# A hybrid decoder layer: half of x turned by the host, small roots moved to VectorE, and a new order of the first weight splits of the last product

## The chip, the cores and the metric

The kernel runs on one core of one Trainium2 chip. The core has five engines that run side by side: TensorE (PE, matrix products and transposes), VectorE (DVE), ScalarE (ACT), GpSimd (POOL) and SyncE (SP, which here only issues transfers). 16 DMA engines move data between the device memory and the on-chip memories SBUF (128 partitions) and PSUM (where TensorE writes). The metric is the device time of one execution in microseconds (us); lower is better. Three runs of the kernel before took 2543.54, 2546.9 and 2548.43 us.

## The reference, cut to what matters

One decoder layer over 2048 tokens of width 1024, all in float32:

```python
h = rms_norm(x, norm1_g)
proj = h @ w_in                       # columns are shared out among three mixers
o_a = swa_sink_mixer(qa, ka, va, ...) # sliding window of 128, learned sinks
o_b = s5_mixer(u, ...)                # complex diagonal state space, 32 groups, GELU and GLU
o_c = nsa_mixer(qc, kvc, gc, ...)     # compressed + selected + window attention, gated
mixed = concat(rms_norm(o_a), rms_norm(o_b), rms_norm(o_c))
x = x + mixed @ w_out
h2 = rms_norm(x, norm2_g)
x = x + relu(h2 @ w_up) ** 2 @ w_down
```

The output is x, 2048 x 1024. `rms_norm` divides by the root of the mean square, so it needs one reciprocal root for each token and part.

## The kernel before, in words

Every product is made from pairs of numbers: an operand is split into a high part that TensorE takes fast (type fp32r) and a low part, the rest. `split` (L1418 to L1421) is the helper: ScalarE casts the high part (L1420), VectorE subtracts it from the source (L1421). A product then is three matmuls: high by high, high by low, low by high.

The order of the instructions on each engine, and of the transfers on each queue, is fixed when the program is built: a planner takes the program in its written order as priority, takes an instruction as soon as its inputs and its buffer are free by its own estimate of times, and can so hoist loads far ahead. `tc.high_priority(offset=n)` moves a block n steps forward in that order. On the chip each engine and each queue runs its list strictly in order, and an instruction that waits holds up all behind it on the same engine or queue.

**`phase_front`** (L81) makes `x @ w_in`. The tokens are taken in 16 tiles of 128 (tile s holds tokens s, s+16, ...). `fetch(s)` loads raw rows (L104). `load_h(s)` turns a tile: eight transposes on TensorE into two PSUM banks (L116), and for each half the split into `hh` (ScalarE, L118) and `hl` (VectorE, L119). The function that it returns squares the raw rows on ScalarE with a sum (L123) and takes the reciprocal root on POOL (L125, in `rsqrt_steps`, L44 to L49: eight small steps, one after another). The root is applied when a product is copied out of PSUM (L172, L176). The 16 tiles go in two halves of eight. Products of the first half come first; then `load_h(8)` to `load_h(15)` are put between the products of chunk `v`, at every second place, and merged with `pair_steps` (L472), which builds tables for the state space mixer: `outer(b)` multiplies on POOL (L483) and VectorE (L484) and adds on POOL (L485); `local(b)` stores the result, makes the small products `pk` (L493) and stores `kst` (L498). Buffers: `ot` has one, `oCA` two, `kst` one, the turned banks two, raw x three. Rows of the finished products for the attention mixers are stored from SP's queue by `store` (L180).

**Attention and the state space mixer** follow. Their bias tables come by `bias_steps`, whose first load is `Ts` (L719), and the weights of the GLU by `glu_steps` (L626), all on SP's queue.

**`phase_mix`** (L1024) is the third mixer, 16 blocks of 128 tokens, and beside it `mixed @ w_out` block by block. `logits` (L860 on) leaves a softmax that POOL scales (L887 on `sls` and `slw`, L1140 on `slc`); `pv` transposes it (L900) and multiplies (L911). `open_late` (L1055) runs once, when the state space mixer is done: it takes the roots `ra` and `rc` of 128x16 sums on POOL, 14 steps each, halves `rc` (L1072), and sends `rc` through memory to turn it. For each block `finish_steps` loads `mix`, scales it on POOL (L1238) and calls `normed` (L934): ScalarE squares with a sum, the root is taken on POOL, and POOL scales (L941). The last block does both on VectorE.

**`phase_up` and `phase_down`** are the FFN. Each product of 2 x 2 blocks is made as seven products instead of eight (Strassen's scheme in Winograd's form); `ORDER = "1675243"` is the order of the seven. `phase_up` ends with combinations on POOL (`ev`, L1582) that are stored to `vd`. `phase_down` (L1667) multiplies `vd` by combinations of `w_down`. For each of eight chunks `weights` makes the differences on POOL (L1723) and `keep` splits the seven weights (`dw`); `tokens(k)` loads the rows for product k from `vd` (L1741) and splits them (`v`). The first chunk's weights and the first five row tiles are written ahead, under high priority, so that they run while `phase_up` ends:

```python
first["0"]()
for k in range(AHEAD):
    tokens(k)
    first[ORDER[k]]()
for o in ORDER[AHEAD:]:
    first[o]()
```

Weights "1" and "6" have a pool of their own (`w_low`), the others share `w_high` (five buffers); rows share `vr` (three raw buffers) and five split buffers. These pools lie where `phase_up` had its own, and each buffer waits for what used its place.

Of the kernel before, what the change touches and what calls it, by code (L numbers as in the profile page):

```python
# [80 lines left out]
def phase_front(tc, C, x, norm1_g, w_in, u_st, pd, rh_a, prm, dkp, dca, pre, extra, done):  # L81

    nc = tc.nc
    with ExitStack() as ctx:
# [14 lines left out]
        r_of, raw_x, hs = {}, {}, {}  # L99

        def fetch(s):
            if s < T16:
                raw_x[s] = xp.tile([P, D], F32, tag="x", name=f"x{s}", bufs=3)
                nc.sync.dma_start(raw_x[s], xv[s])  # L104

        def load_h(s):
# [4 lines left out]
            hs[s] = hh, hl
            for half in range(2):
                pt = ps_t.tile([P, 4, P], F32, tag="pt", name=f"pt{s}_{half}")
                for j in range(4):
                    k = 4 * half + j
                    nc.tensor.transpose(pt[:, j], xt[:, k * P:(k + 1) * P], C["ident"])  # L116
                sl = slice(4 * half, 4 * half + 4)
                nc.scalar.copy(hh[:, sl], pt)  # L118
                nc.vector.tensor_tensor(hl[:, sl], pt, hh[:, sl], op=ALU.subtract)  # L119
# [35 lines left out]
        def product(s, W, ch, k0=0, k1=NK, between=()):  # L155
            kind, c0, n = ch
            hh, hl = hs[s]
            if k0 == 0:
                open_[s, ch] = ps_m.tile([P, n], F32, tag="pm", name=f"pm{s}_{kind}{c0}")
            pm = open_[s, ch]  # L160
            between = list(between)
            for k in range(k0, k1):
                mm3(nc, pm, hh[:, k], hl[:, k], W[k][0], W[k][1], k == 0, k == NK - 1)
                if between:
                    between.pop(0)()
            if k1 < NK:
                return
            if kind == "u":
                r = T16 - 1 - s
                g0 = (c0 - 512) // 16  # L170
                dst = u_st[:, g0:g0 + 16, (r // 8) * P + (r % 8) * 16:(r // 8) * P + (r % 8) * 16 + 16]
                nc.scalar.activation(dst, pm.rearrange("p (g q) -> p g q", q=16), AF.Copy, scale=r_of[s])  # L172
            else:
                f, nh, step = HEADS[kind]
                o = sp.tile([P, n + nh], F32, tag="po", name=f"po{s}_{kind}", bufs=3)
                nc.scalar.activation(o[:, 0:n], pm, AF.Copy, scale=r_of[s])  # L176
                sq = sp.tile([P, 6, 64], F32, tag="sq", name=f"sq{s}_{kind}", bufs=1)[:, 0:nh]
                nc.scalar.activation(sq, o[:, f:f + nh * step].rearrange("p (h d) -> p h d", d=step)[:, :, 0:64], AF.Square)
                nc.vector.tensor_reduce(o[:, n:n + nh], sq, axis=AX.X, op=ALU.add)
                rows.append(lambda: nc.sync.dma_start(pdv[kind][s], o))  # L180
                store(1)
# [290 lines left out]
def pair_steps(tc, C, S, dkp, dca, tp, ps):  # L472
# [5 lines left out]
    def outer(b):  # L478
# [6 lines left out]
        nc.gpsimd.tensor_tensor(CA, CA, t1, op=ALU.add)  # L485
# [361 lines left out]
class Attn:  # L847
# [86 lines left out]
    def normed(self, dst, o, name, eng=None):  # L934
# [5 lines left out]
        rsqrt_into(nc, self.sm, r, ss, 1.0 / 256, 1, "nq", eng)  # L940
# [83 lines left out]
def phase_mix(tc, C, x, gains, B, cmp, w_out, out_norm_g, g2, pd, oa_d, ob, x1, hT, xs, rr, rh, ss_a, ss_b, r_d, rest, release):  # L1024
    nc = tc.nc
    kcA, kcB, vc = cmp
    with ExitStack() as ctx:
# [390 lines left out]
def split(nc, dh, dl, src):  # L1418

    nc.scalar.copy(dh, src)  # L1420
    nc.vector.tensor_tensor(dl, src, dh, op=ALU.subtract)  # L1421
# [245 lines left out]
def phase_down(tc, x1, w_down, vd, out):  # L1667
# [8 lines left out]
    with ExitStack() as ctx:  # L1676
# [12 lines left out]
        acc, V, R = {}, {}, {}  # L1689
# [24 lines left out]
        def weights(c, res):  # L1714
# [20 lines left out]
        def tokens(k):  # L1735
# [7 lines left out]
            split(nc, t[:, 0], t[:, 1], r)  # L1743
# [42 lines left out]
        with tc.high_priority(offset=DOWN_HOIST):  # L1786
# [35 lines left out]
def trunk(tc, x, norm1_g, w_in, qk_g, sinks, rel_bias, a_re, a_im, log_dt, b_re, b_im, c_re, c_im, d_skip, glu_w, glu_b,  # L1822
# [3 lines left out]
    with ExitStack() as ctx:  # L1826
# [38 lines left out]
        phase_front(tc, C, x, norm1_g, w_in, u_st, pd, rh_a, (a_re, a_im, log_dt, b_re, b_im, c_re, c_im, d_skip), dkp, dca,  # L1865
# [93 lines left out]
```

## Time and profile before

| | |
|---|---|
| median of three runs | 2546.9 us |
| the profiled execution, its own time | 2552.13 us |
| its span, first to last instruction | 2550.2 us |
| TensorE busy, matmuls | 2444.3 us, 96% of the span |
| VectorE, ScalarE, GpSimd busy | 1721.8, 1324.6, 1203.2 us |

The same by stage, from the busy time of each engine in stretches of the profile (us):

| stretch | what runs | length | PE | DVE | ACT | POOL | PE clock |
|---|---|---|---|---|---|---|---|
| 0 to 145 | first half of x @ w_in | 145 | 134.89 | 84.02 | 65.90 | 20.23 | 1.00 |
| 145 to 230 | second half turned, pair steps | 85 | 80.29 | 34.85 | 37.92 | 59.88 | 1.00 |
| 230 to 417 | rest of x @ w_in, state space | 187 | 185.72 | 135.32 | 92.85 | 42.46 | 1.00 |
| 417 to 676 | window attention, GLU, compression | 259 | 238.86 | 171.57 | 167.96 | 73.73 | 0.95 |
| 676 to 725 | hand-over inside `phase_mix` | 49 | 37.69 | 30.43 | 28.19 | 23.94 | 0.86 |
| 725 to 1290 | sparse attention and w_out | 565 | 523.50 | 405.39 | 330.86 | 276.36 | 0.97 |
| 1290 to 1929 | first FFN product | 639 | 630.88 | 347.89 | 346.00 | 395.62 | 1.00 |
| 1929 to 2551 | second FFN product | 622 | 612.49 | 512.37 | 254.95 | 310.98 | 0.99 |

How to read the rows further down: a row of the busy view gives a stretch, its length, then for PE, PEld (weight loads), DVE, ACT and POOL the busy time with the number of instructions, the granted clock of TensorE as a share of full speed, the busy share of the DMA engines and the GB/s moved. A row in order of time has the start, the time taken, the engine, the line, the operation, the output and the inputs, how many instructions are merged, and in brackets the idle time before and what ended it. Names are the program's without numbers; L is a line of the kernel before. Matmuls are pipelined, so the time of one is longer than the distance between two.

### The profile page before, as it was taken

The page shows a single profiled execution, that of the slowest core. Times are in us where ns is not written, and L with a number is a line of the kernel's source. Part 1 is how long each engine was busy: PE and PEld are TensorE (multiplying, and loading weights), DVE is VectorE, ACT ScalarE, POOL GpSimd, SP SyncE. Part 2 cuts the span into 40 slices and gives each one's busy share as a digit, 9 for nine tenths or more (in the row PEclk, how much of TensorE's full clock was granted, in tenths as well). Part 3 has the DMA queues.
Part 4 walks back from the last instruction along what each step waited for, and adds up shares of the span by engine and source line. Part 5 has one row for each costly group of instructions (what it writes and reads, how often), then busy time and mean ns, then how long its engine had stood idle before and what let it go on. Part 6 is the DMA issues. An engine that isn't in the chain of part 4 may idle for free.

```text
span 2550.2 us, 38303 instructions
## 1 busy us (share of the span) xinstructions
PE 2444.3 (96%) x12776; PEld 2065.4 (81%) x12776; DVE 1721.8 (68%) x3424; ACT 1324.6 (52%) x2767; POOL 1203.2 (47%) x1263
## 2 busy tenths in 40 slices
PE   8999999899989999899999999999999999999999
PEld 8989997677778878788778787788887888888887
DVE  4743884775587787677554545745457888888886
ACT  6334545675576566555455555654554444334442
POOL 3045222223445354454646666666554444545447
PEclk9999999998999999999999999999999999999999
DMA  6153425311121112131656677755547534444335
GB/s 200 61 127 96 125 87 163 97 58 49 44 92 51 57 51 68 55 98 55 198 193 189 191 198 210 227 160 155 148 121 261 164 102 126 133 132 132 120 101 197
DMA packets 397174, 324.65 MB, mean 127 GB/s; under 512 B 51974, under 2 KB 363916, under 8 KB 395152
## 3 DMA queue, kind: packets, MB, share of 16 engines
q1 hardware_dynamic: 360880, 297.03, 39.2%
q10 hardware_dynamic: 36096, 25.17, 3.1%
q8 instruction: 101, 1.65, 0.3%
q14 instruction: 97, 0.79, 0.1%
HBM read 209.66 MB, written 112.45 MB: 126 GB/s over the span
## 4 chain that ended last, share of the span: by engine, by line
PE 63%; DVE 5%; DMA 3%; POOL 3%; issue 3%; ACT 2%; SPq 0%; ACTq 0%; DVEq 0%; POOLq 0%
PE pdc L1755 7%; PE pdb L1755 7%; PE pda L1755 7%; PE pub L1566 6%; PE puc L1566 6%; PE pua L1566 6%; PE pdd L1755 3%; PE pud L1566 3%; PE poc L911 3%; PE pps L900 2%; PE pw L76 2%; PE pw L77 2%; PE pw L78 2%; PE pqs L876 1%; PE pqs L877 1%
## 5 line engine op out<-in xcount | busy, mean ns | idle before, releaser
L1420 ACT CAST v<-vr 128x512 fp32r<-128x512 f32 x224 | 139.4, 624 | 305.4 <-DMA vr<-vd 142.9
L1421 DVE TENSOR_TENSOR v<-vr,v 128x512 fp32r<-128x512 f32 x224 | 233.7, 1052 | 78.2 <-ACT v L1420 77.9
L1755 PE MATMUL pdc<-dw,v 128*128 128x512 f32 x768 | 187.4, 393 | 4.1 <-ACT dw L1420 3.2
L1755 PE MATMUL pda<-dw,v 128*128 128x512 f32 x768 | 184.5, 389 | 0.0
L1755 PE MATMUL pdb<-dw,v 128*128 128x512 f32 x768 | 184.5, 389 | 0.0
L1537 POOL TENSOR_TENSOR fs<-ur,ur 128x512 f32<-128x512 f32 x64 | 92.9, 1452 | 176.4 <-DMA ur<-in_w_up 131.2
L1755 PEld LDWEIGHTS pdc<-dw,v 128*128 128x128 f32 x768 | 145.5, 190 | 35.8 <-ACT dw L1420 3.6
L1755 PEld LDWEIGHTS pdb<-dw,v 128*128 128x128 f32 x768 | 144.2, 188 | 30.0
L1755 PEld LDWEIGHTS pda<-dw,v 128*128 128x128 f32 x768 | 144.1, 188 | 30.0
L1421 DVE TENSOR_TENSOR ul<-ur,uh 128x512 fp32r<-128x512 f32 x96 | 93.3, 972 | 109.8 <-ACT uh L1420 109.7
L1421 DVE TENSOR_TENSOR ul<-fs,uh 128x512 fp32r<-128x512 f32 x128 | 133.7, 1048 | 33.9 <-ACT uh L1420 33.9
L1420 ACT CAST uh<-fs 128x512 fp32r<-128x512 f32 x128 | 78.2, 621 | 141.7 <-PE pub L1566 56.4
L887 POOL TENSOR_SCALAR sls<-sls,dens,gt 128x128 f32<-128x128 f32 (+15 forms) x64 | 81.7, 1277 | 105.8 <-DVE dens L886 85.7
L903 ACT CAST ths<-pps 128x512 fp32r<-128x512 f32 (+1 forms) x144 | 79.8, 560 | 79.6 <-PE poc L911 58.1
L904 DVE TENSOR_TENSOR tls<-pps,ths 128x512 fp32r<-128x512 f32 (+1 forms) x144 | 93.8, 658 | 38.7 <-ACT ths L903 34.1
L76 PE MATMUL pw<-wo_h,mh 128*128 128x512 f32 x256 | 109.7, 428 | 7.6 <-ACT mh L1250 5.8
L900 PE MATMUL pps<-c_ident,sls 128*128 128x128 f32 x544 | 103.0, 281 | 9.1 <-POOL sls L887 5.4
L1582 POOL TENSOR_TENSOR ev<-e,e 128x512 f32<-128x512 f32 x64 | 98.3, 1535 | 27.9 <-ACT e L1579 16.8
L887 POOL TENSOR_SCALAR slw<-slw,denw,gt 128x640 f32<-128x640 f32 (+4 forms) x64 | 52.9, 827 | 122.1 <-DVE denw L886 98.5
L78 PE MATMUL pw<-wo_h,ml 128*128 128x512 f32 x256 | 105.0, 411 | 2.1 <-DVE ml L1251 2.1
L77 PE MATMUL pw<-wo_l,mh 128*128 128x512 f32 x256 | 106.4, 416 | 0.0
L1566 PE MATMUL puc<-fh,uh 128*128 128x512 f32 x256 | 101.0, 395 | 5.3 <-DVE eu L1575 5.3
(562 smaller groups left out, 7960.6 us busy)
## 6 DMA issues: line engine op xcount, KB each, us to landing
vr<-vd SPq DMA_DIRECT2D x224, 256.0 KB
ur<-in_w_up SPq DMA_DIRECT2D x128, 256.0 KB
vd<-ev SPq DMA_DIRECT2D x128, 256.0 KB
vd<-e ACTq DMA_DIRECT2D x64, 256.0 KB
dr<-in_w_down SPq DMA_DIRECT2D x32, 512.0 KB
x<-in_x SPq DMA_DIRECT2D x16, 512.0 KB
mx<-in_x SPq DMA_DIRECT2D x16, 512.0 KB
x<-mx ACTq DMA_DIRECT2D x16, 512.0 KB
```

Source lines behind the costliest of these rows:

```text
L76: nc.tensor.matmul(out, sh, mh, start=first, stop=False)
L77: nc.tensor.matmul(out, sh, ml, start=False, stop=False)
L78: nc.tensor.matmul(out, sl, mh, start=False, stop=last)
L887: nc.gpsimd.tensor_scalar(x, x, den[:, h:h + 1], gate, op0=ALU.mult, op1=ALU.mult)
L900: nc.tensor.transpose(pt[:, j, hh], sls[hh][:, (b0 + j) * P:(b0 + j + 1) * P], C["ident"])
L904: nc.vector.tensor_tensor(tl[:, 0:nb], pt[:, 0:nb], th[:, 0:nb], op=ALU.subtract)
L1420: nc.scalar.copy(dh, src)
L1421: nc.vector.tensor_tensor(dl, src, dh, op=ALU.subtract)
L1537: nc.gpsimd.tensor_tensor(t, x, y, op=op)
L1566: nc.tensor.matmul(bank[b], w[:, k], h[o][:, k], start=first and k == 0 and n == 0, stop=k == HALF - 1 and n == 2, skip_group_check=True)
L1582: nc.gpsimd.tensor_tensor(tile_("v" + o), x, y, op=op)
L1755: nc.tensor.matmul(bank[b, q], x[:, q, j], y[:, j], start=first and j == 0 and n == 0, stop=j == 1 and n == 2, skip_group_check=True)
```

## The change

1. The host passes a second copy of x, tiles 8 to 15 only, already turned: eight blocks of 128 x 8 x 128. `fetch` loads both forms for these tiles, and `load_h` splits from the turned SBUF tile and makes no transposes. A pool `a_x2` holds three turned and two raw tiles; it is opened after the tables of the state space mixer and closed before `done()`.
2. The roots of tiles 8 to 15 are taken on VectorE instead of POOL.
3. The stores of the c rows of tiles 8 to 15 are issued from ScalarE's queue instead of SP's.
4. In `pair_steps` the addition of `CA` moves from POOL to VectorE.
5. The roots in `normed` (all blocks) and the two in `open_late`, with the halving of `rc`, move from POOL to VectorE. The scaling by the root stays where it was.
6. In `phase_down` the first weights and rows are written in the order 1 t0 6 7 t1 5 t2 2 t3 4 t4 3 (t is a tile of rows), and the split of t3 is ordered behind the two instructions of weight "7", on ScalarE and on VectorE each.

```diff
         def fetch(s):
             if s < T16:
-                raw_x[s] = xp.tile([P, D], F32, tag="x", name=f"x{s}", bufs=3)
+                if s >= 8:
+                    turned_x[s] = late_p[0].tile([P, NK, P], F32, tag="xt", name=f"xt{s}", bufs=3)
+                    nc.sync.dma_start(turned_x[s], xt_in[s - 8])
+                raw_x[s] = (late_p[0] if s >= 8 else xp).tile([P, D], F32, tag="x", name=f"x{s}", bufs=2 if s >= 8 else 3)
                 nc.sync.dma_start(raw_x[s], xv[s])
...
+                if s >= 8:
+                    pt = turned_x[s][:, sl]
+                else:
+                    pt = ps_t.tile([P, 4, P], F32, tag="pt", name=f"pt{s}_{half}")
+                    for j in range(4):
+                        k = 4 * half + j
+                        nc.tensor.transpose(pt[:, j], xt[:, k * P:(k + 1) * P], C["ident"])
...
-                rsqrt_into(nc, xp, r, ss, 1.0 / D, 1, "rq", nc.gpsimd)
+                rsqrt_into(nc, xp, r, ss, 1.0 / D, 1, "rq", nc.vector if s >= 8 else nc.gpsimd)
...
-                rows.append(lambda: nc.sync.dma_start(pdv[kind][s], o))
+                rows.append(lambda: (nc.scalar if s >= 8 and kind == "c" else nc.sync).dma_start(pdv[kind][s], o))
...
+        c_x = ctx.enter_context(ExitStack())
+        late_p.append(c_x.enter_context(tc.tile_pool(name="a_x2", bufs=1)))
...
-        nc.gpsimd.tensor_tensor(CA, CA, t1, op=ALU.add)
+        nc.vector.tensor_tensor(CA, CA, t1, op=ALU.add)
...
-        rsqrt_into(nc, self.sm, r, ss, 1.0 / 256, 1, "nq", eng)
+        rsqrt_into(nc, self.sm, r, ss, 1.0 / 256, 1, "nq")
...
-            rsqrt_into(nc, sm, ra, ss_a, 1.0 / 256, NT, "ra", nc.gpsimd)
-            rsqrt_into(nc, sm, rc, ss_b, 0.25 / 512, NT, "ra", nc.gpsimd)
-            nc.gpsimd.tensor_scalar(rc, rc, 0.5, 1.0, op0=ALU.mult, op1=ALU.mult)
+            rsqrt_into(nc, sm, ra, ss_a, 1.0 / 256, NT, "ra")
+            rsqrt_into(nc, sm, rc, ss_b, 0.25 / 512, NT, "ra")
+            nc.vector.tensor_scalar(rc, rc, 0.5, None, op0=ALU.mult)
...
+            with ExitStack() as behind:
+                if k == 3:
+                    for i in lead["7"]:
+                        behind.enter_context(tc.issue_after(i.ins))
+                split(nc, t[:, 0], t[:, 1], r)
...
-            for k in range(AHEAD):
-                tokens(k)
-                first[ORDER[k]]()
-            for o in ORDER[AHEAD:]:
-                first[o]()
+            for e in "1 t0 6 7 t1 5 t2 2 t3 4 t4 3".split():
+                tokens(int(e[1])) if e[0] == "t" else first[e]()
```

More of the change, by code (lines that the diff above doesn't have):

```diff
@@ L78, in mm3, with phase_front @@
     nc.tensor.matmul(out, sl, mh, start=False, stop=last)
-def phase_front(tc, C, x, norm1_g, w_in, u_st, pd, rh_a, prm, dkp, dca, pre, extra, done):
+def phase_front(tc, C, x, xt_in, norm1_g, w_in, u_st, pd, rh_a, prm, dkp, dca, pre, extra, done):
     nc = tc.nc
@@ L98, in phase_front @@
         g1 = sm.tile([P, NK], F32, tag="g1", name="g1", bufs=1)
-        r_of, raw_x, hs = {}, {}, {}
+        r_of, raw_x, turned_x, hs, late_p = {}, {}, {}, {}, []
         def fetch(s):
             if s < T16:
-                raw_x[s] = xp.tile([P, D], F32, tag="x", name=f"x{s}", bufs=3)
+                if s >= 8:
+                    turned_x[s] = late_p[0].tile([P, NK, P], F32, tag="xt", name=f"xt{s}", bufs=3)
+                    nc.sync.dma_start(turned_x[s], xt_in[s - 8])
+                raw_x[s] = (late_p[0] if s >= 8 else xp).tile([P, D], F32, tag="x", name=f"x{s}", bufs=2 if s >= 8 else 3)
                 nc.sync.dma_start(raw_x[s], xv[s])
@@ L112, in load_h @@
             for half in range(2):
[L113 to L116, printed above, removed]
                 sl = slice(4 * half, 4 * half + 4)
+                if s >= 8:
[5 more added lines that the diff above has]
+                        nc.tensor.transpose(pt[:, j], xt[:, k * P:(k + 1) * P], C["ident"])
                 nc.scalar.copy(hh[:, sl], pt)
@@ L244, in phase_front @@
         run(merge(body, pairs))
+        c_x.close()
         done()
@@ L1418, in split @@
 def split(nc, dh, dl, src):
-    nc.scalar.copy(dh, src)
-    nc.vector.tensor_tensor(dl, src, dh, op=ALU.subtract)
+    return (nc.scalar.copy(dh, src), nc.vector.tensor_tensor(dl, src, dh, op=ALU.subtract))
 def phase_up(tc, C, x1, rr, g2, hT, xs, w_up, vd):
@@ L1688, in phase_down @@
         ps = pool("d_ps", 2, space=PSUM)
-        acc, V, R = {}, {}, {}
+        acc, V, R, lead = {}, {}, {}, {}
         places = [(m, n) for m in range(8) for n in ("u", "22", "11", "21", "12")]
@@ L1727, in keep @@
                 t = (w_low if o in ORDER[:2] else w_high).tile([P, 2, 2, N], F32R, tag="w", name=f"dw{c}{o}")
-                split(nc, t[:, 0], t[:, 1], src)
+                lead[o] = split(nc, t[:, 0], t[:, 1], src)
                 res[o] = t[:, 0], t[:, 1]
@@ L1742, in tokens @@
             t = (v_high if k % 6 else v_low).tile([P, 2, 2, 2, P], F32R, tag="v", name=f"v{c}{g}{ORDER[o]}")
-            split(nc, t[:, 0], t[:, 1], r)
+            with ExitStack() as behind:
[3 more added lines that the diff above has]
+                split(nc, t[:, 0], t[:, 1], r)
             V[k] = t[:, 0], t[:, 1]
@@ L1819, in phase_down, with trunk @@
                 w = nw
-def trunk(tc, x, norm1_g, w_in, qk_g, sinks, rel_bias, a_re, a_im, log_dt, b_re, b_im, c_re, c_im, d_skip, glu_w, glu_b,
+def trunk(tc, x, x_t, norm1_g, w_in, qk_g, sinks, rel_bias, a_re, a_im, log_dt, b_re, b_im, c_re, c_im, d_skip, glu_w, glu_b,
           cmp_pos, cmp_w1, cmp_w2, out_norm_g, w_out, norm2_g, w_up, w_down,
@@ L1864, in trunk @@
         pre = c_pre.enter_context(tc.tile_pool(name="pre", bufs=1, side="right"))
-        phase_front(tc, C, x, norm1_g, w_in, u_st, pd, rh_a, (a_re, a_im, log_dt, b_re, b_im, c_re, c_im, d_skip), dkp, dca,
+        phase_front(tc, C, x, x_t, norm1_g, w_in, u_st, pd, rh_a, (a_re, a_im, log_dt, b_re, b_im, c_re, c_im, d_skip), dkp, dca,
                     pre, late_loads, c_pre.close)
@@ L1947 @@
     arrays, args = {}, []
-    host = {n: inputs[n] for n in _INS}
+    host = {}
+    for n in _INS:
+        host[n] = inputs[n]
+        if n == "x":
+            host["x_t"] = _np.asarray(inputs[n])[0].reshape(P, T16, NK, P).transpose(1, 3, 2, 0)[8:]
     host.update(_shape_constants())
```

## The prediction

> **What bounds the kernel now.** I read the page's busy shares first, then the busy time by stage, then what TensorE (PE) waited for, then single stretches in order of time. Two rows of the page:
>
> ```profile
> span 2550.2 us, 38303 instructions
> PE 2444.3 (96%) x12776; PEld 2065.4 (81%) x12776; DVE 1721.8 (68%) x3424; ACT 1324.6 (52%) x2767; POOL 1203.2 (47%) x1263
> ```
>
> PE idles 106 us in all, so an edit pays if it takes work off PE, closes one of these gaps, or avoids the lowered clock behind one. By stage (columns: PE, PEld, VectorE = DVE, ScalarE = ACT, GpSimd = POOL busy, granted clock, DMA share, GB/s), and the waits at the edited places (total, times, longest):
>
> ```profile
> 162.00:203.00 41.00, 36.54 (x273) 33.84 (x272) 15.51 (x29) 21.54 (x45) 33.59 (x62) 1.00 0.38 118
> 676.00:725.00 49.00, 37.69 (x202) 31.23 (x202) 30.43 (x81) 28.19 (x67) 23.94 (x61) 0.86 0.37 109
> 725.00:1290.00 565.00, 523.50 (x3207) 444.40 (x3206) 405.39 (x1172) 330.86 (x766) 276.36 (x460) 0.97 0.25 80
> PE pt L116 <- DVE hl L119: 4.5, 4, 2.1
> PE pm_u L76 <- ACT u_st L172: 2.2, 2, 1.9
> PE bpfs L712 <- DMA Ts<-rs: 2.2, 1, 2.2
> PE pps L900 <- POOL sls L887: 5.4, 1, 5.4
> PE ppc L900 <- POOL slc L1140: 4.4, 1, 4.4
> PE pdc L1755 <- ACT dw L1420: 3.2, 1, 3.2
> PE pth L1283 <- DVE mx L1263: 6.8, 5, 1.8
> ```
>
> The edits touch four places: the turning-in of x tiles 8 to 15 (162 to 203 us), the hand-over to attention (400 to 426), the mixing phase (676 to 1290), and the start of the second FFN product (1929 on).
>
> **Part 1, tiles 8 to 15 turned by the host, and two POOL jobs given to DVE.** One period on PE, then what POOL and DVE do in such a period:
>
> ```profile
> 195.31 1.04 PE L116 MATMUL pt<-c_ident,x 128*128 128x128 f32 x8
> 196.18 1.03 PE L493 MATMUL pk<-oCA,k_Y 128*128 128x256 f32 x4
> 199.78 0.28 PE L78 MATMUL pm_u<-wh_u,hl 128*128 128x256 f32 x1
> 169.50 1.17 POOL L483 TENSOR_TENSOR oCA<-k_AR,k_C 128x544 f32<-128x544 f32 x1
> 170.74 1.35 POOL L485 TENSOR_TENSOR oCA<-oCA,ot 128x544 f32<-128x544 f32 x1
> 172.18 0.72 POOL L44 TENSOR_SCALAR rqh<-ss 128x1 f32<-128x1 f32 x1
> 175.56 1.18 POOL L483 TENSOR_TENSOR oCA<-k_AR,k_C 128x544 f32<-128x544 f32 x1
> 172.12 0.73 DVE L484 TENSOR_TENSOR ot<-k_AI,k_C 128x544 f32<-128x544 f32 x1 [4.04 <-POOL oCA L485]
> 172.77 1.28 DVE L119 TENSOR_TENSOR hl<-pt,hh 128x512 fp32r<-128x512 f32 x2
> 173.97 0.17 DVE L496 TENSOR_TENSOR kst<-pk,k_dD 16x32 f32<-16x32 f32 x1
> ```
>
> Eight transposes hold PE 196.18 - 195.31 = 0.87 us; 8 tiles make 7.0 us removed. The waits of 4.5 and 2.2 us hang on POOL: its loop takes 175.56 - 169.50 = 6.06 us a tile, 3.4 of it the root (172.18 to 175.56). DVE stands behind it for 4.04 us, and the subtracts that free the transposes' bank stand behind that. Both waits lose their cause: at best 7.0 + 6.7 = 13.7 us.
>
> What DVE takes on, priced by the one such root already there and by subtracts of two SBUF inputs (the sources are no longer PSUM):
>
> ```profile
> L44 DVE TENSOR_SCALAR nqh<-ns x1: 153/153/153, 1260.2 to 1260.2; 128x1 f32<-128x1 f32 x1
> L49 DVE TENSOR_SCALAR nr<-nqt,nr x3: 214/214/215, 1260.9 to 1262.0; 128x1 f32<-128x1 f32 x3
> 1905.05 0.69 DVE L1421 TENSOR_TENSOR ul<-ur,uh 128x512 fp32r<-128x512 f32 x1 [2.65 <-ACT uh L1420]
> 1907.38 1.41 DVE L1421 TENSOR_TENSOR ul<-ur,uh 128x512 fp32r<-128x512 f32 x1
> ```
>
> A root runs from 1260.2 to 1262.0 + 0.2: 2.0 us. The add has the shape of L484, 0.73 us (up to POOL's 1.35). A subtract costs 0.69 to 1.41 against 0.64 now. DVE's work per tile goes from 0.73 + 1.28 + 0.17 = 2.2 to 2.2 + 2.0 + 0.73 = 4.9 us, or 4.9 + 0.6 + 1.5 = 7.0 with both upper ends. PE without transposes needs 199.9 - 196.18 = 3.7 us a tile. So DVE is the slower by 1.2 us a tile, 9.6 over eight. The halves hide it (tile 8 is used five products after its turn, later tiles with more), the products pk do not: they need the sum from one pair step earlier, a lead of about 3.7 us. So 9.6 - 3.7 = 5.9 shows: gain 13.7 - 5.9 = 7.8, taken as **8**. Ends: 13.7 gained; or eight tiles at 7.0 = 56 us instead of 41, 15 lost. I stay near the low price because POOL is left only 1.2 us of each period.
>
> The Trainium skill, "SBUF — State Buffer", section Who interferes with whom, speaks against this: a VectorE instruction with two SBUF inputs contends with a GpSimd instruction that reads SBUF, and whoever issues second blocks. By the 0.69 row the sum stays; by the rule at its fullest it is the 1.41 row, and that is a rival below.
>
> Eight more issues on SP bring 8 x 0.5 = 4.2 MB. The stretch moved 118 x 41 = 4.8 MB; 9.0 MB in some 35 us would be 257 GB/s. This row says that the queues can carry it, nearly full:
>
> ```profile
> 440.00:450.00 10.00, 9.22 (x52) 6.30 (x51) 9.45 (x31) 9.83 (x34) 3.72 (x3) 1.00 0.85 222
> ```
>
> I cost it at nothing, hidden behind products; where it is late, the stores of kst, on the same queue, are late next, and DVE's next kst behind them. The raw rows now have two buffers, so a fetch waits on SP for a square one tile back.
>
> **Part 2, stores of the c rows on ACT's queue.**
>
> ```profile
> 399.78 7.70 SPq L180 DMA_DIRECT2D pc<-po_c  x2
> 407.53 0.91 SPq L626 DMA_DIRECT2D graw<-in_glu_w  x2
> 413.99 0.38 SPq L719 DMA_DIRECT2D Ts<-rs  x1
> 422.00:424.00 2.00, 1.60 (x5) 0.60 (x4) 0.00 (x0) 0.94 (x2) 0.39 (x1) 0.50 0.99 313
> ```
>
> SP stands for 7 us before the second store; behind it queue the GLU weights, then Ts, for which PE waits 2.2 us and then runs at half clock. Free of the stores SP can be earlier. Whether the buffers are free then no row says: 0 to 2.2 + 1.0 (half clock over that row) gained, up to 8 x 0.38 = 3 us lost if ACT, which issues the eight stores now, issues as slowly as SP's row for Ts and all of it falls on the path. I take **2** gained.
>
> **Part 3, roots of the mixing phase on DVE.**
>
> ```profile
> 688.85 0.20 POOL L44 TENSOR_SCALAR rah<-ss_b 128x16 f32<-128x16 f32 x1 [3.63 <-ACT gb L671]
> 698.62 0.77 POOL L887 TENSOR_SCALAR sls<-sls,dens,gt 128x512 f32<-128x512 f32 x1
> 718.22 0.45 POOL L1140 TENSOR_TENSOR slc<-slc,wc 128x160 f32<-128x160 f32 x1
> ```
>
> The softmax scaling at 698.62 stands behind almost 10 us of small POOL steps, slc behind the steps of one normalising root: the waits of 5.4 and 4.4. The clock of 0.86 over 49 us costs 6.9 more. On DVE the 29 steps of r_a and r_c at 0.15 to 0.27 are 4 to 8 us, in a DVE 62% busy there: one queue of steps is exchanged for a shorter one. Of 16.7 I take **5** gained (0 to 14). Afterwards only the price is left: 15 roots of 2.0 us, 30 us more in a DVE that is 405/565 = 72% busy; the longest wait of PE there is on DVE (the pth row), none on POOL's roots. What shows lies between PE's idle share (41.5 of 565 us, 7%) and those 72%; I take 10%, **3** lost (2 to 21).
>
> **Part 4, third weights ahead of the fourth rows.**
>
> ```profile
> 1931.52 2.88 PE L1755 MATMUL pdd<-dw,v 128*128 128x512 f32 x12
> 1937.59 1.22 PE L1755 MATMUL pdc<-dw,v 128*128 128x512 f32 x2 [3.19 <-ACT dw L1420]
> 1939.43 4.42 PE L1755 MATMUL pdc<-dw,v 128*128 128x512 f32 x10 [0.62 <-DVE dw L1421]
> 1952.42 2.88 PE L1755 MATMUL pdb<-dw,v 128*128 128x512 f32 x12
> 1928.69 1.66 ACT L1420 CAST v<-vr 128x512 fp32r<-128x512 f32 x3 [0.44 <-ACT e L1579]
> 1937.72 1.04 ACT L1420 CAST dw<-dt 128x1024 fp32r<-128x1024 f32 x1 [0.19 <-POOL ev L1582]
> ```
>
> A product takes 2.72 us. The second ends at 1934.24, the seventh would end 5 x 2.72 later, at 1947.84; it ends at 1955.14: 7.3 us lost, of which the wait is 3.8, and 10 matmuls in 4.42 us show half clock. With the third weights cast ahead of the fourth rows (second or third of the casts at 1928.69) they are there by 1934. Late next are the fourth product's weights, cast at 1937.72 behind POOL, their low half near 1940, against a due time of 1937: 3 us stay. Gain **4** (7.3 to 1.5 lost). The fourth rows wait on ACT and DVE; behind them stand later rows and SP's load into their buffer, due about 11 us later.
>
> The Trainium skill, "TensorE: Matmul & The Clock Gate", section What's actually happening, lowers the clock after an idle window of about 3.4 us; a rest of 3 us would then keep full clock, while the 2.2 us wait of part 2 has half clock behind it. By the rule the gain is 4, by that row nearer 2.
>
> **Sum.** -8 - 2 - 5 + 3 - 4 = -16 us. The profiled execution took 2552.1 (span 2550.2, 1.9 around it), 5.2 above the median of 2546.9; so 2546.9 - 16 = **2531**.
>
> **Rivals.**
> *All gaps close*, with their clock: -13.7 - 3 - 14 + 2 - 7.3 = -36, 2511. For it: POOL, the cause of most, is idle afterwards. Against: DVE takes over its queue. 0.12.
> *VectorE paces the turning-in* (the skill's port rule, priced by rows): with subtracts of 1.0 instead of 0.69 a tile takes 5.5 us, eight take 44, less the lead of 3.7 just under today's 41, and part 1 gains 1 to 2; part 4's buffer is free only when POOL's ev ends, gain 1: -1.5 - 2 - 5 + 3 - 1 = -6.5, 2540. For it: 4.9 against 3.7. 0.18.
> *Given back*: the same, and 30% of the 30 us shows (9 instead of 3): -0.5, 2546. 0.14.
> *Slower: DVE bounds the mixing phase.* 72% of the 30 us, and r_a's steps exchange nothing: -8 - 2 + 0 + 21 - 4 = +7, 2554. It decides once more than 14/30, 47%, shows. For it: the pth row, PE's longest wait in the stretch. Against: PE is idle for 7% of it in all. 0.10.
> The forecast has the remaining 0.46.
>
> **Range and chances.** 0.2%, 5 us, is what a measurement of this kernel can tell from no change. Faster: 0.46 + 0.12 + 0.18 = 0.76; same 0.14; slower 0.10. From 2513, nearly the first rival, to 2549, past the given-back case, about 0.1 is left out on each side; the forecast alone is 2523 to 2537.
>
> **What would show it.** Right: no L116 work on PE after 100 us, products about 3.7 to 4.5 us apart, no 4.5 and 2.2 us waits; Ts issued before 412; the sls and slc waits below 2 us and the clock of that stage above 0.93; pdc waiting under 1 us, pdb then up to 3. Wrong: pk waiting for DVE L485, kst waiting for its store for several us, PE waits on DVE in the mixing phase well over today's, the third weights' cast still near 1936.

## The result and the profile after

The changed kernel takes 2512.5 us (median of four runs, 2508.4 to 2514.3), the kernel before, run beside it, 2547.7 us. The ratio is 0.9858, with a 95% interval of 0.9834 to 0.9882: 36 us saved (30 to 42), where 16 were forecast. The time lies 0.5 us below the range. The profiled execution took 2511.4 us. Its page:

```profile
span 2509.6 us, 38157 instructions
PE 2428.8 (97%) x12712; PEld 2051.5 (82%) x12712; DVE 1754.9 (70%) x3653; ACT 1325.4 (53%) x2767; POOL 1118.8 (45%) x1034
```

TensorE (PE) idles 80.8 us instead of 105.9, and is busy 15.5 us less. Only 7 of these are the removed transposes; for the rest the granted clock is the likely cause, 0.989 over the span against 0.984 (0.5% of 2444 us is 12). By stretch (columns as in the prediction; the second and third stretch begin about 18 us earlier than the two shown of before, since the same work comes earlier):

```profile
162.00:203.00 41.00, 38.90 (x289) 36.95 (x289) 34.68 (x98) 23.53 (x47) 13.70 (x10) 1.00 0.68 229
658.00:707.00 49.00, 43.39 (x231) 35.73 (x229) 40.43 (x137) 32.45 (x76) 14.32 (x18) 0.86 0.43 133
707.00:1250.00 543.00, 513.92 (x3194) 434.78 (x3193) 412.95 (x1269) 326.34 (x761) 247.98 (x356) 0.99 0.25 81
```

The waits at the edited places, from the view of what PE waited for (us in total, times, longest):

```profile
PE pth L1292 <- DVE mx L1272: 5.0, 4, 1.6
PE pqw L885 <- DVE nmc L888: 3.4, 2, 2.3
PE pdb L1767 <- DVE v L1429: 2.0, 1, 2.0
PE pdc L1767 <- ACT dw L1429: 1.6, 1, 1.6
PE pk L502 <- DVE r L49: 1.2, 1, 1.2
```

The waits of 5.4 (`sls`), 4.4 (`slc`), 5.2 (`tls`) and 4.5 us (`pt`) are gone, and the one of 5.2 us for `mh` has shrunk to 1.2. In order of time, the load of `Ts` on SP's queue, and PE at the start of the last product:

```profile
402.45 0.38 SPq L728 DMA_DIRECT2D Ts<-rs  x1
...
1888.74 2.91 PE L1767 MATMUL pda<-dw,v 128*128 128x512 f32 x12
1891.48 2.88 PE L1767 MATMUL pdd<-dw,v 128*128 128x512 f32 x12
1895.98 0.73 PE L1767 MATMUL pdc<-dw,v 128*128 128x512 f32 x2 [1.62 <-ACT dw L1429]
1897.39 2.56 PE L1767 MATMUL pdc<-dw,v 128*128 128x512 f32 x10 [0.67 <-DVE dw L1429]
1899.78 0.84 PE L1767 MATMUL pdb<-dw,v 128*128 128x512 f32 x3
1902.58 3.92 PE L1767 MATMUL pdb<-dw,v 128*128 128x512 f32 x9 [1.96 <-DVE v L1429]
1906.31 2.94 PE L1767 MATMUL pda<-dw,v 128*128 128x512 f32 x12
```

Where the 40.6 us between the two spans went, by the starts of the same instructions: 9.7 are gained by the last product of the front (`pm_c`), 7.7 more by the first transposes of the mixing phase (`ptx`, at 705.3 before and 687.9 after), 23.7 more by the first product of the FFN (`pua`, 1290.8 and 1249.7); the two FFN products together give 0.5 back. So the mixing phase, from which 2 us had been expected, is the largest part.

### The profile page after: what moved, and what is told of

It reads as the page before. It is cut to its first block, busy times and chain, and to the rows that moved or that the text cites. A ratio compares the mean times of both kernels' runs of the same rounds, so it can differ in the third digit from the quotient of the medians.

```text
span 2509.6 us, 38157 instructions
## 1 busy us (share of the span) xinstructions
PE 2428.8 (97%) x12712; PEld 2051.5 (82%) x12712; DVE 1754.9 (70%) x3653; ACT 1325.4 (53%) x2767; POOL 1118.8 (45%) x1034
## 5 line engine op out<-in xcount | busy, mean ns | idle before, releaser
L1574 PE MATMUL pub<-fh,uh 128*128 128x512 f32 x256 | 103.2, 403 | 4.0 <-DVE e L1583 4.0
L1590 POOL TENSOR_TENSOR ev<-e,e 128x512 f32<-128x512 f32 x64 | 92.2, 1441 | 27.0 <-ACT e L1587 16.4
```

The source lines that it names most:

```text
L1574: nc.tensor.matmul(bank[b], w[:, k], h[o][:, k], start=first and k == 0 and n == 0, stop=k == HALF - 1 and n == 2, skip_group_check=True)
L1590: nc.gpsimd.tensor_tensor(tile_("v" + o), x, y, op=op)
```

## The experiments

Below, "saved" is (1 - ratio) x 2547 us, with its interval. "Mixing phase" is the length from the first `ptx` to the first `pua` of a profiled run.

**The four parts, one at a time, and the mixing roots taken out.** `only_mix_roots` is the kernel before with

```diff
-        rsqrt_into(nc, self.sm, r, ss, 1.0 / 256, 1, "nq", eng)
+        rsqrt_into(nc, self.sm, r, ss, 1.0 / 256, 1, "nq")
...
-            rsqrt_into(nc, sm, ra, ss_a, 1.0 / 256, NT, "ra", nc.gpsimd)
-            rsqrt_into(nc, sm, rc, ss_b, 0.25 / 512, NT, "ra", nc.gpsimd)
-            nc.gpsimd.tensor_scalar(rc, rc, 0.5, 1.0, op0=ALU.mult, op1=ALU.mult)
+            rsqrt_into(nc, sm, ra, ss_a, 1.0 / 256, NT, "ra")
+            rsqrt_into(nc, sm, rc, ss_b, 0.25 / 512, NT, "ra")
+            nc.vector.tensor_scalar(rc, rc, 0.5, None, op0=ALU.mult)
```

> The kernel before with part 3 alone: the roots in normed and the two in open_late, with the halving, on VectorE. Theory A (the roots on POOL held up the softmax scalings and the w_out input, and PE behind them, all through the mixing phase): the whole -24 us that the mixing phase gained shows here, 2520 to 2528 us, and the waits of 5.4 (sls), 4.4 (slc) and 5.2 (tls) are gone. Rival B (the mixing phase gained because the planner, given other times by the other parts, happened on a better order): this part alone gives what the prediction took for it, 0 to -6 us, 2541 to 2547.

`all_but_mix_roots` is the changed kernel with these lines as before.

> The changed kernel with part 3 undone: the roots of normed and open_late back on POOL. Theory A: the mixing phase loses its 24 us again, 2534 to 2540 us, with stalls of 4 to 5 us behind POOL's softmax scaling. Rival B: within 6 us of the changed kernel, 2510 to 2519.

`only_front` is the kernel before with the host-turned tiles, their roots on VectorE and `nc.vector` in the addition to `CA`.

> The kernel before with part 1 alone: tiles 8 to 15 turned by the host, their roots and the addition to CA on VectorE; stores, mixing phase and last product as before. Theory A: the gain is the front stretch's own, -10 us, 2535 to 2540, and from 500 us on the distances are those of before. Rival B: more than 15 us are gained, the surplus in the mixing phase, 2525 to 2532.

`only_down_order` is the kernel before with the new order "1 t0 6 7 t1 5 t2 2 t3 4 t4 3" and the fourth rows ordered behind the weights "7".

> The kernel before with the new order of the first weight splits and rows of the last product alone. From the two traces: the lead of 4 us at the second product is handed back by the end. Both theories on the mixing phase: within 3 us of the kernel before, 2544 to 2549. The prediction's part 4 had -4 us, 2542 to 2545; if its 4 us are really kept, the time is at most 2544.

| kernel | median us | ratio, interval | saved us | mixing phase us |
|---|---|---|---|---|
| only_mix_roots | 2525.9 | 0.9917, 0.9903 to 0.9931 | 21 (18 to 25) | 567.1 |
| all_but_mix_roots | 2534.4 | 0.9945, 0.9933 to 0.9958 | 14 (11 to 17) | 584.0 |
| only_front | 2541.2 | 0.9969, 0.9958 to 0.9980 | 8 (5 to 11) | 584.5 |
| only_down_order | 2546.2 | 1.0001, 0.9991 to 1.0010 | 0 (-3 to 2) | 584.4 |
| before | | | | 585.5 |
| changed | 2512.5 | 0.9858, 0.9834 to 0.9882 | 36 (30 to 42) | 561.8 |

Theory A's times came (`only_front` lies 1 us above its range): 21 of the 36 us are the mixing roots, alone as well as taken out (36 - 14 = 22), and the mixing phase moves with them and with nothing else. That the *other* parts had shifted it (rival B) is refuted. The new order of the last product is worth nothing.

**Which of the roots.** `only_normed_roots` has the first of the lines above, `only_open_late_roots` the rest.

> The kernel before with the roots of normed on VectorE alone; the two of open_late stay on POOL. The whole part 3 gave -21 us. Theory A1 (the 15 roots of normed, spread over the mixing phase, each delay POOL's softmax scaling by 3.5 us): most of it, -14 to -21 us, 2526 to 2533. Theory A2 (the 10 us of steps in open_late delay the hand-over to the w_out products once, and the gain is that one delay): 0 to -5, 2542 to 2547.

> The kernel before with the two roots of open_late and the halving on VectorE alone; the roots of normed stay on POOL. Theory A1: 0 to -6 us, 2541 to 2547, the 4.4 us wait for slc and the 5.2 us wait for tls stay, only that of 5.4 us for sls goes. Theory A2: -14 to -21 us, 2526 to 2533.

Measured: normed alone 2534.3 us, ratio 0.9953 (0.9937 to 0.9968), 12 us saved; open_late alone 2541.7 us, ratio 0.9984 (0.9973 to 0.9996), 4 us saved. The sum, 16, leaves some 5 of the 21 to both together. Theory A1 is the nearer one, though its range of 2526 to 2533 is missed by 1 us: most of the gain lies in the 15 roots to which the prediction had given a loss.

How a root on POOL could cost that much is seen in the kernel before at one place; POOL, VectorE and PE in order of time:

```profile
1057.21 0.19 POOL L44 TENSOR_SCALAR nqh<-ns 128x1 f32<-128x1 f32 x1
...
1060.63 0.26 POOL L49 TENSOR_SCALAR nr<-nqt,nr 128x1 f32<-128x1 f32 x1
1060.86 0.69 POOL L1238 TENSOR_SCALAR mix<-mix,r_b 128x512 f32<-128x512 f32 x1
1061.53 0.47 POOL L941 TENSOR_SCALAR mix<-oc,nr 128x256 f32<-128x256 f32 x1
1061.99 0.87 POOL L887 TENSOR_SCALAR slw<-slw,denw,gt 128x640 f32<-128x640 f32 x1
1062.82 0.93 POOL L1139 TENSOR_TENSOR pn<-slc,denc 128x448 f32<-128x448 f32 x1
...
1063.79 0.93 DVE L1147 TENSOR_REDUCE pm<-pn 128x112 f32<-128x448 f32 x1 [5.07 <-POOL pn L1139]
1064.63 1.28 DVE L904 TENSOR_TENSOR tls<-pps,ths 128x512 fp32r<-128x512 f32 x2
...
1065.37 0.79 PE L911 MATMUL poc<-tls,Vs 128*128 128x256 f32 x2 [5.21 <-DVE tls L904]
```

PE's wait of 5.21 us carries VectorE's name. VectorE itself had stood for 5.07 us at `pm`, which needs `pn` from POOL, and on POOL `pn` stood behind the root of a block. The low half `tls`, which was ready to be made, stood behind `pm` on VectorE's list. The view of VectorE's own waits has the whole of it:

```profile
DVE pm L1147 <- POOL pn L1139: 9.0, 4, 5.1
```

The prediction did not read this view; it read only PE's waits, in which POOL is not named for this stall.

In the profiled runs just over half of normed's gain in the mixing phase lies at this one place. Counted from `ptx` by the starts of the same PE instructions, the profiled run of `only_normed_roots` is level with the kernel before at 1057.4 us (0.1 behind), 7.7 us ahead at 1069.5, 8.7 at 1180 and 14.8 at `pua`; the last 6 come after 1260, where PE's waits for `mh` and `ml` fall from 5.8 and 2.1 us to 3.1 and 1.6. The stretch from 1057.4 to 1069.5 takes 11.2 to 12.1 us in the seven kernels that keep these roots on POOL in the order of before, and 4.3 to 4.4 us in `only_normed_roots`, `only_mix_roots`, the changed kernel and its variants. Two things changed there at once: on POOL no root of `normed` stands ahead of `pn` any more, and on VectorE `denc` (which `pn` needs as well) and `pm` stand behind three more low halves than before.

**Is it POOL's time, the length of the chain, or the order?** `normed_roots_on_both` adds to `only_normed_roots` the same eight steps on POOL, into a tile that nobody reads:

```diff
+        rsqrt_into(nc, self.sm, r, ss, 1.0 / 256, 1, "nq")
+        if eng is nc.gpsimd:
+            idle = self.small(1, "nx")
+            rsqrt_into(nc, self.sm, idle, ss, 1.0 / 256, 1, "nz", eng)
```

> The kernel before with the 15 roots of normed on VectorE, and the same eight steps each on POOL as well, into a tile that nobody reads (extra work, the result of the kernel does not use it). Without the idle steps it was 12 us faster than before. Theory (POOL's occupied time is the cause: what stands behind the root on POOL's queue is late, then VectorE and PE): the gain is lost, 2543 to 2552. Rival (the planner's other order, or the root's own delay, is the cause): the gain stays, 2532 to 2537.

`normed_roots_idle_on_vector` exchanges the two: POOL's root is used as before, VectorE's is idle.

```diff
         rsqrt_into(nc, self.sm, r, ss, 1.0 / 256, 1, "nq", eng)
+        if eng is nc.gpsimd:
+            idle = self.small(1, "nx")
+            rsqrt_into(nc, self.sm, idle, ss, 1.0 / 256, 1, "nz")
```

> The kernel before with idle roots: POOL makes the 15 roots of normed and the scaling reads them, as before; VectorE makes the same 15 roots into a tile that nobody reads (extra work). Every engine's and queue's list has the same operations in the same order as in normed_roots_on_both (2533.8 us); only the reader of the two roots is exchanged. Theory O (the order of the lists is the cause, and the kernel before merely had an unlucky one): 2531 to 2537. Theory L (the scaled rows wait for the slower chain on POOL): the gain is lost, 2544 to 2552.

`normed_roots_long_on_vector` is `only_normed_roots` with six refining turns instead of three.

> The kernel before with the roots of normed on VectorE as in only_normed_roots (2534.3 us), but with six refining turns instead of three, so that each root takes 14 steps, some 3.5 us, about what POOL takes (the result is the same to rounding). Theory L (the length of the chain is the cause): the gain is lost, 2542 to 2550. Theory O (the order, or POOL's queue, is the cause, not the chain): it stays, less up to 4 us for 22 us more of VectorE, 2532 to 2539.

Measured: on both 2533.8 us, ratio 0.9954 (0.9939 to 0.9969); idle on VectorE 2535.9, ratio 0.9967 (0.9955 to 0.9979); long on VectorE 2527.7, ratio 0.9942 (0.9926 to 0.9957). The mixing phases of before, of the first and of the second of these, from the busy view:

```profile
705.30:1290.80 585.50, 538.26 (x3277) 456.32 (x3277) 420.40 (x1202) 342.67 (x790) 284.73 (x475) 0.97 0.26 81
```
```profile
699.60:1273.30 573.70, 535.78 (x3282) 454.72 (x3282) 430.12 (x1317) 344.76 (x795) 281.05 (x475) 0.98 0.26 83
```
```profile
700.10:1271.20 571.10, 533.70 (x3283) 452.47 (x3282) 429.70 (x1317) 344.03 (x794) 280.55 (x475) 0.98 0.26 84
```

POOL does the same 475 instructions in all three, and VectorE 115 more in the last two, and yet these are 12 and 14 us shorter. With POOL as busy as before, 12 us are saved; with a chain as long as POOL's, 15 (11 to 19); and 8 (5 to 11) even where the scaling reads POOL's root, as it did before. These are theory O's numbers, not theory L's: there are orders of the lists in which POOL's busy time, a chain as long, or POOL's root in use do not cost the 12 us.

But the three kernels do not keep the order of `only_normed_roots`, since the planner orders anew for each added step. Of PE's 2411 list rows of the mixing phase before (equal neighbours merged), 124 cannot be matched in the same order in `only_normed_roots` and 146 in the changed kernel, but 655 in the first two of the three and 618 in the third. So what POOL's time would cost in the order of `only_normed_roots`, or of the changed kernel, they do not show. Between the first two the comparison is close: the lists of PE, VectorE and ScalarE in the mixing phase are the same, and on POOL only the scaling stands one to six places earlier in 11 blocks of `normed_roots_idle_on_vector`.

At the place shown above this kernel has the whole root on POOL ahead of `pn`, as before, and yet no stall:

```profile
1049.11 0.27 POOL L49 TENSOR_SCALAR nr<-nqt,nr 128x1 f32<-128x1 f32 x1
...
1051.69 0.94 POOL L1142 TENSOR_TENSOR pn<-slc,denc 128x448 f32<-128x448 f32 x1 [0.90 <-DVE denc L1136]
...
1052.66 0.97 DVE L1150 TENSOR_REDUCE pm<-pn 128x112 f32<-128x448 f32 x1 [0.38 <-POOL pn L1142]
```

POOL is done with the root and stands 0.90 us for `denc`; before, `denc` was there at 1057.5, 5.3 us ahead of `pn`. VectorE's wait for `pn` in the whole phase, in either:

```profile
DVE pm L1150 <- POOL pn L1142: 4.8, 6, 1.8
```

It is spread over six places, and none is longer than 1.8 us. So another order alone removes the stall, with the root still on POOL and in use. Whether taking the root off POOL would remove it in the old order was not tried. How normed's 12 us in `only_normed_roots` are shared between POOL's freed time and the new order is therefore open, and so is what the 4 us (12 - 8) are, since the two intervals overlap.

It is not chance from the other parts: in the seven kernels with these roots on POOL as before (before, all_but_mix_roots, and those with parts 1, 2 and 4 alone or in pieces) PE's list of the mixing phase is one and the same, and it takes 583.9 to 585.8 us; in the five with part 3 whole it is one and the same other list, 561.8 to 570.8 us in six profiled runs. Whether POOL's roots in exactly the changed kernel's order would be as fast as VectorE's was not tried.

**The front in pieces.** `only_host_turned` has the turned tiles, with roots and addition on POOL; `only_front_engines` has those two on VectorE, with the transposes still made.

```diff
-                rsqrt_into(nc, xp, r, ss, 1.0 / D, 1, "rq", nc.gpsimd)
+                rsqrt_into(nc, xp, r, ss, 1.0 / D, 1, "rq", nc.vector if s >= 8 else nc.gpsimd)
...
-        nc.gpsimd.tensor_tensor(CA, CA, t1, op=ALU.add)
+        nc.vector.tensor_tensor(CA, CA, t1, op=ALU.add)
```

> The kernel before with the host-turned tiles alone: the roots of tiles 8 to 15 and the addition to CA stay on POOL. Part 1 whole gave -6 us. Theory: POOL's loop of 6.06 us a tile still paces the pair steps, so the 7 us of transposes become waits of the products pk for the sum: 0 to -3 us, 2544 to 2547. Rival: PE has other products to put between, and the 7 us of transposes are the gain: -5 to -7, 2540 to 2542.

> The kernel before with the roots of tiles 8 to 15 and the addition to CA on VectorE alone; tiles still turned by TensorE. Theory: the 4.5 and 2.2 us waits go, the transposes stay: -2 to -6 us, 2541 to 2545. Rival: VectorE, with 4.9 us of work in a tile, frees the transposes' banks later than today: 0 to +6, 2547 to 2553.

Turned tiles alone: 2548.3 us, ratio 1.0009 (0.9997 to 1.0020), no gain. The engines alone: 2539.8 us, ratio 0.9968 (0.9955 to 0.9980), 8 us, as much as both and a little over what theory had. Neither rival came. The same stretch in the first and in the second:

```profile
162.00:203.00 41.00, 31.38 (x204) 29.11 (x203) 13.94 (x24) 19.89 (x40) 36.83 (x63) 0.92 0.52 175
```
```profile
162.00:203.00 41.00, 41.00 (x323) 39.88 (x322) 35.89 (x108) 24.94 (x51) 11.08 (x10) 1.00 0.41 134
```

Without transposes, but with POOL's loop, PE is busy for 31.4 of 41 us at a clock of 0.92, and waits for POOL's sum:

```profile
PE pk L502 <- POOL oCA L494: 9.6, 5, 3.2
PE pk L502 <- ACT kst L506: 3.2, 1, 3.2
```

Seven microseconds of transposes had been cover for POOL's 6.06 us a tile; taken away they become waits, and more than that: in this profile the front ends at 423.1 us, against 416.3 before. With the engines changed PE is busy for all 41 us.

**Stores of the c rows, and two parts taken out of the changed kernel.** `only_c_stores` has the one line of the stores in the kernel before; `changed_c_on_sync` is the changed kernel without it; `changed_not_turned` the changed kernel without the host-turned tiles; `changed_again` the changed kernel itself on the chip of these two.

```diff
-                rows.append(lambda: nc.sync.dma_start(pdv[kind][s], o))
+                rows.append(lambda: (nc.scalar if s >= 8 and kind == "c" else nc.sync).dma_start(pdv[kind][s], o))
```

> The kernel before with the stores of the c rows of tiles 8 to 15 issued by ScalarE alone. The four parts run so far leave 6 to 8 us for it (2512.5 against 2546.9 is -34; -21 and -6 and 0 are accounted for). Theory: Ts lands before PE needs it, the 2.2 us wait and the half clock behind it go, and the hand-over to attention gains 6 to 8 us, 2539 to 2541. Rival (the prediction's -2; the rest belongs to the parts together, the stores leaving SP just as the turned tiles load it): 2543 to 2547.

> The changed kernel with the stores of the c rows back on SyncE's queue. Alone they gained 4 us. Theory (the 2.2 us wait for Ts and the half clock behind it come back): 4 to 6 us slower than the changed kernel, 2516 to 2519. Rival (beside eight turned tiles on the same queue the stores matter more): 7 to 10 us slower, 2519 to 2523. The prediction's part 2: 2 us slower, 2514 to 2515.

> The changed kernel without the host-turned tiles: TensorE turns tiles 8 to 15 as before, all else as changed. Theory from the single runs (turned tiles alone 0 to +2.6 us, roots and addition alone -6, both -6): within 4 us of the changed kernel, 2510 to 2516. The prediction's reasoning (7 us of transposes off PE, of which some 5.9 show again behind VectorE): 1 us slower than changed. Rival (with POOL out of the way the transposes count in full): 2517 to 2520.

> The changed kernel itself, on the same chip as the three others of this call, so that differences of 3 us can be read. Expected 2510 to 2515.

| kernel | median us | ratio, interval | saved us |
|---|---|---|---|
| only_c_stores | 2542.3 | 0.9985, 0.9972 to 0.9999 | 4 (0 to 7) |
| changed_c_on_sync | 2521.3 | 0.9899, 0.9882 to 0.9916 | 26 (21 to 30) |
| changed_not_turned | 2519.5 | 0.9890, 0.9873 to 0.9908 | 28 (23 to 32) |
| changed_again | 2508.7 | 0.9850, 0.9834 to 0.9866 | 38 (34 to 42) |

Alone the stores lie between theory and rival. In the changed kernel the stores are worth 38 - 26 = 12 us and the turned tiles 38 - 28 = 10, more than alone (4 and 0), though with some 6 us of noise on each difference this is barely clear for the stores. Both rivals' times came. Part of it is seen: with the stores on SP beside the turned tiles the wait for `Ts` is 3.3 us, longer than before the change.

```profile
PE bpfs L721 <- DMA Ts<-rs: 3.3, 1, 3.3
PE bpf L721 <- DMA T<-r: 2.3, 1, 2.3
```

And without turned tiles the front ends 3.5 us later (last `pm_c` at 409.3 against 405.8). `changed_c_on_sync` is 5.4 us behind the changed kernel's own profile by 451 us. The rest of both differences arises later, for `changed_not_turned` with the same list on PE (5.1 us of it in the mixing phase, 570.8 against 565.7), and such stretches differ by as much from run to run (last section). It stays open.

**The order at the last product.** In the changed kernel the fourth product waits 1.96 us for its rows. VectorE and POOL there:

```profile
1898.51 3.42 DVE L1429 TENSOR_TENSOR dw<-dr,dw 128x1024 fp32r<-128x1024 f32 x1
1901.85 0.68 DVE L1429 TENSOR_TENSOR v<-vr,v 128x512 fp32r<-128x512 f32 x1
1902.45 1.21 DVE L1429 TENSOR_TENSOR dw<-dt,dw 128x1024 fp32r<-128x1024 f32 x1
...
1897.41 3.43 POOL L1731 TENSOR_TENSOR dt<-dr,dt 128x1024 f32<-128x1024 f32 x1 [1.16 <-DVE dw L1429]
```

`changed_fourth_rows_first` puts the fourth rows ahead of the weights "2":

```diff
-            for e in "1 t0 6 7 t1 5 t2 2 t3 4 t4 3".split():
+            for e in "1 t0 6 7 t1 5 t2 t3 2 4 t4 3".split():
```

> The changed kernel with one exchange in the order of the last product's first splits: the fourth rows (t3) before the weights "2", on ScalarE and VectorE. Theory (the lead of 3.9 us at the fourth product is lost because VectorE subtracts the weights "2", 3.42 us, ahead of the fourth rows): the wait of 1.96 us and the half clock behind it go, the fifth product starts some 14 us after the first instead of 17.6, and 2 to 4 us are kept: 2508 to 2511. Rival (the fifth product is held by its own weights at the same time): the start of the fifth product stays at 17 to 18 us, 2512 to 2513.

Measured: 2509.8 us, ratio 0.9850 (0.9833 to 0.9867), the same as `changed_again`. PE, VectorE and POOL at that place:

```profile
1889.78 0.73 PE L1767 MATMUL pdc<-dw,v 128*128 128x512 f32 x2 [1.62 <-ACT dw L1429]
1891.19 4.00 PE L1767 MATMUL pdc<-dw,v 128*128 128x512 f32 x10 [0.67 <-DVE dw L1429]
1894.99 3.13 PE L1767 MATMUL pdb<-dw,v 128*128 128x512 f32 x12
1898.23 3.01 PE L1767 MATMUL pda<-dw,v 128*128 128x512 f32 x12
...
1892.31 2.86 DVE L1429 TENSOR_TENSOR v<-vr,v 128x512 fp32r<-128x512 f32 x1
...
1891.21 3.41 POOL L1731 TENSOR_TENSOR dt<-dr,dt 128x1024 f32<-128x1024 f32 x1 [1.16 <-DVE dw L1429]
```

The wait is gone, and the fifth product starts 15.7 us after the first instead of 17.6, not 14: ten matmuls of the third now ran at half clock (4.00 instead of 2.56 us). By the last matmul 0.9 us of it are left, too little for the whole time to show. And the slow subtract has moved: now the rows' one takes 2.86 instead of 0.68 us, while the weights' takes its usual 1.2. In both kernels it is the one that runs beside POOL's subtract, and it ends 0.5 to 1.1 us after POOL does (1901.93 after 1900.84, 1895.17 after 1894.62).

**The next step on the same way.** `changed_plus_x1_roots` moves the last 16 roots of the mixing phase, those of the new x rows, to VectorE as well; `changed_plus_x1_roots_and_add` also the addition ahead of each.

```diff
-                    nc.gpsimd.tensor_tensor(ss, box["ss"][:, 0:1], box["ss"][:, 1:2], op=ALU.add)
-                    rsqrt_into(nc, sm, rr[:, i:i + 1], ss, 1.0 / D, 1, "xr", nc.gpsimd)
+                    nc.vector.tensor_tensor(ss, box["ss"][:, 0:1], box["ss"][:, 1:2], op=ALU.add)
+                    rsqrt_into(nc, sm, rr[:, i:i + 1], ss, 1.0 / D, 1, "xr")
```

> The changed kernel with the last roots on POOL, the 16 of the new x rows in the mixing phase (the rows' mean squares for the second norm), on VectorE as well. If POOL's queue is still what delays PE there (theory A carried on): another 5 to 15 us gained, 2498 to 2508. If POOL's share was used up and VectorE, 72% busy before and busier now, is next: same to 8 us slower, 2512 to 2520.

> The changed kernel with the 16 roots of the new x rows on VectorE, and with them the addition of the two half sums ahead of each, which stayed on POOL in the run that was 13 us slower. Theory (there VectorE stood up to 3.9 us for POOL's addition, and the low halves for TensorE behind it): most of the 13 us come back, 2508 to 2518. Rival (VectorE is simply full with 16 more roots): still 2522 to 2528.

Measured: 2525.2 us, ratio 0.9927 (0.9905 to 0.9949), and 2522.6 us, ratio 0.9893 (0.9867 to 0.9919): both slower than the changed kernel. VectorE's and PE's waits at the end of the mixing phase of the first:

```profile
DVE xrh L44 <- POOL xq L1279: 6.4, 5, 3.9
```
```profile
PE ptx L1257 <- DVE ml L1260: 6.2, 2, 4.9
```

VectorE stood for POOL's addition, as theory had it. But with the addition moved too, and that wait gone, the mixing phase takes 577.8 us in both. The theory that most of the loss would come back falls. The rival's time (2522 to 2528) came, but that VectorE is full is not shown: it is busy for 450.6 of the 577.8 us. What costs these 16 us against 561.8 in the second was not tracked down: its order is a new one again, and PE is busy 541.6 us there against 531.1, at a lower clock.

## Why the prediction was right or wrong

**Sum and sign.** Faster was right (0.76), -16 was less than half of -36. The time is that of the first rival, "all gaps close" (2511), but not by its terms: it had -13.7, -3, -12 and -7.3 for the four parts, and measured alone they are -8, -4, -21 and 0.

**Part 1, -8: measured 8 (5 to 11).** The size is right, in part by luck; the working is only half right. The two waits did hang on POOL. But the 7.0 us of transposes were not a gain to which the waits are added: alone the turned tiles gained nothing, and the two jobs moved to VectorE gained the whole 8. By the end of the front in the profiled runs (last `pm_c`, 416.3 before) the two jobs alone gain 8.0 us (408.3), the turned tiles on top of them 3.1 (405.2), and alone they lose 6.8 there (423.1). So 7.0 gained by the transposes was too much, 5.9 lost to VectorE's queue was too much as well, and the two errors work against each other. VectorE's price for one instruction held: `hl` from SBUF took 0.68 us in the median, as the low price of 0.69 had it, and the products `pk` waited 1.2 us for VectorE's root, once. "VectorE paces the turning-in" therefore did not come; the port rule of the Trainium skill ("SBUF — State Buffer", Who interferes with whom) hardly bit here: the longest of 14 such subtracts took 1.38 us. POOL, which was left little to read, was busy for 13.7 of 41 us, 33.6 before.

**Part 2, -2: measured 4 (0 to 7) alone.** `Ts` was issued at 402.45, as the sign list wanted (before 412), and its wait went. In the changed kernel the same edit is worth 12, above the end of 3.2; turned tiles and stores share SP's queue, and the sum treated them as apart.

**Part 3, -5 + 3 = -2: measured 21 (18 to 25). This is the step that failed.** Its first term, 5 for `open_late`, is right: 4 (1 to 7) alone. Its second, "Afterwards only the price is left: 15 roots of 2.0 us", has the wrong sign: 12 (8 to 16) gained where 3 were to be lost. The step took POOL's roots as harmless after 725 us because PE's view names no wait on them there; the wait stood under VectorE's name, one engine further back, and that one place is worth 7 to 8 us. It also took the `pth` row for the longest wait there; that row is the largest sum (6.8 us), but none of its five waits is over 1.8 us, and the longest single ones were the 5.2 us for `tls` and the 5.2 us for `mh`. And it priced the edit as so many steps moved, where the planner also orders the lists anew, which no price of steps can give; what each of the two is worth is open. The sign list was half wrong as well: the `sls` and `slc` waits went, but the clock of that stage stayed at 0.86.

**Part 4, -4: measured 0 (-3 to 2).** The third weights came earlier as worked out (`pdc` waits 1.62 instead of 3.19, then 0.67 as before), and the fourth product started 3.9 us sooner after the first (11.04 against 14.91). "3 us stay" named the fourth *weights* as late next. In their place it was the fourth *rows*: VectorE's subtract of the weights "2" ahead of them took 3.42 us, PE waited 1.96 and ran nine matmuls at half clock (3.92), and the fifth product started as late as before (17.57 and 17.64 after the first). The sentence that the rows wait on ACT and DVE was there; the wait had no number.

## What to carry to other kernels

Where PE waits for an engine, look at that engine's own waits before the cause is named: the engine in the row may itself be standing, in order, behind a third one for something PE does not need. Work is worth taking off the busiest engine only when nothing else paces the stretch; taken off first, it turns into waits and a lower clock. And where a planner fixes the order, moving a small instruction is two changes, its price and a new order. An idle copy of the instruction can show that an order is enough, but it moves the order again: compare the lists before two such kernels are compared.

## What the runs showed of the hardware that had not been expected

**Half clock without a long wait.** The kernel before, in the stretch from 600 us on:

```profile
600.00:602.00 2.00, 1.73 (x11) 1.15 (x10) 1.58 (x14) 1.37 (x8) 1.30 (x4) 1.00 0.00 0
602.00:604.00 2.00, 2.00 (x9) 1.74 (x8) 1.41 (x10) 1.78 (x8) 1.66 (x4) 0.51 0.31 73
...
612.00:614.00 2.00, 2.00 (x9) 1.71 (x7) 0.81 (x7) 0.89 (x4) 0.45 (x1) 0.50 0.00 0
```

PE's longest wait from 590 to 620 us:

```profile
PE pqw L877 <- DVE kBw L1109: 0.6, 1, 0.6
```

The granted clock stays at one half for some 13 us, from 602 on, with PE busy all the time. In `only_down_order`, whose lists are the same up to the last product, the same stretch has full clock, and 96 instead of 81 matmuls are done in 20 us:

```profile
600.00:610.00 10.00, 8.87 (x49) 6.83 (x49) 8.34 (x41) 7.76 (x32) 5.45 (x11) 1.00 0.21 59
610.00:620.00 10.00, 9.14 (x47) 7.07 (x46) 4.45 (x19) 5.18 (x18) 2.82 (x6) 1.00 0.13 47
```

By the starts of the same PE instructions the kernel before is 3.4 us behind at 600 us and 7.9 at 616, so this stretch cost it 4.5 us; runs of one kernel differ by up to 10 (2540.6 to 2550.6 in 18 runs). The changed kernel's profile has such a stretch too (0.50 from 590 to 595 us), that of `changed_again` has none. The Trainium skill ("TensorE: Matmul & The Clock Gate", What's actually happening) lowers the clock after an idle window of about 3.4 us; no such idle time stands ahead of this stretch.

**VectorE stands until a POOL instruction ends.** The 3.42 and 2.86 us above, for subtracts that take 1.2 and 0.68 alone, end 1.1 and 0.5 us after POOL's subtract, about the time that they take alone. That is the port rule of the Trainium skill cited above, two SBUF inputs against POOL's reads, and here the trace agrees with it.
